# Output projection with the token blocks standing and the weight columns moving

## The chip, the cores and the metric

The kernel runs on one core of one Trainium2 chip. The metric is the device time of one execution in microseconds (us). Three runs of the kernel before took 1353.34, 1355.34 and 1359.38 us; the median is 1355.34. Each number of the trace below comes from one further execution, which was profiled and took 1355.63 us.

The engines are named as in the profile: PE is the matrix engine (PEld its weight loads), DVE the vector engine, ACT the scalar engine, POOL the general one, SP the one that issues most transfers. A matmul has a *standing* operand, which PEld loads into the array, and a *moving* operand, which is streamed through it column by column. A sum of matmuls grows in a PSUM bank (512 fp32 values in each of 128 partitions) and has to be copied out by DVE or ACT.

## What is computed

One decoder layer for a prompt of 512 tokens and a sample group of 32 tokens (8 sequences of 4) with the same weights. An input projection feeds two groups of 8 attention heads each; the heads' outputs, each times a SiLU gate, are joined and go through one output projection, are added to the residual, and are normalised. The part that the change touches:

```python
def merge(x, o_n, z_n, o_f, z_f, w_out):
    mix = jnp.concatenate([o_n * jax.nn.silu(z_n), o_f * jax.nn.silu(z_f)], axis=-1)
    return x + jnp.einsum('btc,cd->btd', mix, w_out)
...
def rmsnorm(x, g):
    xf = x.astype(jnp.float32)
    y = xf * lax.rsqrt(jnp.mean(xf * xf, axis=-1, keepdims=True) + RMS_EPS)
    return (y * g.astype(jnp.float32)).astype(x.dtype)
...
    y_prompt = rmsnorm(hp, norm_final)
    y_sample = rmsnorm(hs, norm_final)
```

`mix` has 2048 columns (16 heads of 128), `w_out` is 2048 by 2048, all in fp32.

## The kernel before

**Precision.** A product of two fp32 matrices is made of three matmuls in the faster type fp32r. Each operand is split into a high part, rounded by a copy on ACT, and a low part, the difference, made by DVE. `mm3` (line 366) issues high x high, high x low and low x high. For the activations the parts are `h_hi` and `h_lo`, [128, 16, 544]: features over the partitions, 16 blocks k of 128 features, and 544 = 512 + 32 tokens. For the weights they are `whi` and `wlo`.

**Projections.** `run_tiles` (452) handles a list of tiles. A tile is 128 columns of a weight matrix, loaded in four pieces of 512 rows (`w_dma`, 417, a ring of five `raw` buffers, 256 KB each) and split two pieces ahead (`w_split`, 437). The weights stand and the tokens move: 544 tokens are cut into two halves of 272 (`cuts`), each half with a PSUM bank of its own (`pz`), and each piece brings 4 k x 3 matmuls to each half. So a tile is 96 matmuls of 272 moving columns, and its result has output features over the partitions and tokens along the row. The evicted result is `zt`, and a generator per tile (`post`) carries on with it.

**Order.** The program is written out by one loop over the tiles, which calls `S.pump()` after every few matmuls. The pump lets the other pieces of work (attention, mixing, eviction) issue their instructions as soon as a model of the engines' clocks, `Clock` (40), thinks that they would not have to wait. Each engine executes its own instructions in that written order. The `Streams` items wait on flags such as `in_done`.

**From the heads to the output.** `post_z` (1605) applies SiLU to a gate tile and leaves it in `mx[:, hd]`. `mix` (1618) multiplies it by the head's output, the prompt part read from `oz`, the sample part from `o_s` [128, 16, 32]. `turn_in` (1634) splits a finished head into `h_hi[:, hd]` and `h_lo[:, hd]`, in place of the input activations, and so waits for `in_done`, the end of all input tiles. The last 16 of the input tiles are the gates z0 to z15.

**Output projection.** Ten tiles of the usual form, then the last six tile columns twice: once for token rows 256 to 543 (288 columns) and once for rows 0 to 255 (`N_TWO = 6`, lines 1742 to 1748), so that half of the tokens can be finished and stored while the other half is still computed. `post_y` (1643) turns each result on PE (five transposes, or three, or two, into `tr` banks), so that tokens lie over the partitions, adds the residual `xr` into `res` [128, 5, 2048] on DVE, sums the squares on ACT, and multiplies by the norm's weight `nfb`. `finish` (1685) forms the root (`rstd_of`, 1712: two operations and four steps of three) for all of a half's token blocks and scales their rows, on DVE and ACT. `store_one` (1708) stores 512 columns of 128 tokens (256 KB) on SP: one store at each weight load for the first half, and the eight of the second half at the end.

Of the kernel before, what the change touches and what calls it, by code (L numbers as in the profile page):

```python
# [1 line left out]

# [5 lines left out]
F32 = mybir.dt.float32  # L8
F32R = mybir.dt.float32r
# [5 lines left out]
P = 128  # L15
# [3 lines left out]
KT = 16  # L19
# [5 lines left out]
N_TWO = 6  # L25
# [248 lines left out]
def trunk_step(ctx, tc, x_prompt, x_sample, cache_nsa_kv, cache_fox_kv, cache_fox_logf, state_nsa_win,  # L274
# [139 lines left out]
    raws, wsp, later = {}, {}, []  # L414
    W_RAW, W_AHEAD = 5, 2

    def w_dma(m):
        t, c = divmod(m, 4)
        if t >= len(tiles):
            return  # L420
        spec = tiles[t]
        raws[m] = raw = wts.tile([P, 4, P], F32, name="raw", bufs=W_RAW)
        src = spec["w"]
        ld = src.shape[-1]
        c = spec.get("rows", (0, 1, 2, 3))[c]
        for (col, n, at) in spec["cols"]:
            nc.sync.dma_start(raw[:, :, at:at + n], dram(src, c * 4 * P * ld + col, [[ld, P], [P * ld, 4], [1, n]]))
        if later:
            store_one()

        b, part = divmod(m - 4 * T_WIN, 4)
        if 0 <= b < 8:
            at = (b * 512 + part * 127) * 512
            nc.sync.dma_start(dram(nsa_win_sample, at, [[512, 127], [1, 512]]),
                              dram(state_nsa_win, at + 4 * 512, [[512, 127], [1, 512]]))

    def w_split(m, part):
        t, c = divmod(m, 4)
        if t == 0 or t >= len(tiles):
            return  # L440
        n = tiles[t]["m"]
        raw = raws[m][:, :, :n]
        if part == 0:
            wsp[m] = [wts.tile([P, 4, P], F32R, name=w, bufs=W_AHEAD + 1) for w in ("whi", "wlo")]
            cp(wsp[m][0][:, :, :n], raw)
        else:
            low(*(x[:, :, :n] for x in wsp[m]), raw)
            del raws[m]
            if m > 4:
                w_dma(m - 1 + W_RAW)  # L450

    def run_tiles(t0, t1):
        for t in range(t0, t1):
# [8 lines left out]
            cuts = spec.get("cuts", ((0, HALF), (HALF, TOK)))  # L462
            ps = [psum.tile([P, b - a], F32, name="pz", tag="pz", bufs=2) for a, b in cuts]
            raw_part = []
            if t >= n_in:
                spec["post"].ahead()
            for c in range(4):
# [19 lines left out]
                if "rows" in spec:  # L487
                    S.need(*[f"h{spec['rows'][c] * 4 + kk}" for kk in range(4)])
                for hf, cut in enumerate(cuts):
                    sl = slice(*cut)  # L490
                    for kk in range(4):
                        k = spec.get("rows", (0, 1, 2, 3))[c] * 4 + kk
                        mm3(ps[hf][:n], (hi[:, kk, :n], lo[:, kk, :n]), (h_hi[:, k, sl], h_lo[:, k, sl]),
                            c == 0 and kk == 0, c == 3 and kk == 3)
                        if kk == 3 and c == 3:

                            if 1 < t < n_in:
                                S.need("rsb")
                            elif t == 1:
                                raw_part.append(sl)  # L500
                            late = max(clock.t["dve"], clock.t["pe"]) > max(clock.t["act"], clock.t["pe"]) + 0.2
                            if not 1 < t < n_in:
                                (cp if late else nc.vector.tensor_copy)(zt[:n, sl], ps[hf][:n])
                            elif late:
                                cp(zt[:n, sl], ps[hf][:n])
                                raw_part.append(sl)
                            else:
                                nc.vector.tensor_tensor(zt[:n, sl], ps[hf][:n], rsb[:n, sl], op=OP.mult)
                        if hf == len(cuts) - 1 and kk % 2 == 0:
                            w_split(m + W_AHEAD, kk // 2)  # L510
                        S.pump()
# [13 lines left out]


# [1091 lines left out]
    def mix(hd):  # L1618
# [12 lines left out]
        nc.vector.tensor_tensor(m[:, SEQ:], m[:, SEQ:], o_s[:, hd, :], op=OP.mult)  # L1631
        flags.add(f"mix{hd}")

    def turn_in(hd):
        yield (f"mix{hd}", "in_done")
        m = MX["mx"][:, hd, :]
        cp(h_hi[:, hd, :], m)
        yield
        low(h_hi[:, hd, :], h_lo[:, hd, :], m)
        flags.add(f"h{hd}")  # L1640


    def post_y(n, r0=0, r1=4, smp=True):

        nr = r1 - r0

        got = []

        def ahead():
            if fin and not got:  # L1650
                got.append(load(fin.tile([P, 4, P], F32, name="xr", bufs=2)[:, :nr],
                                dram(x_prompt, r0 * P * D + n * P, [[D, P], [D * P, nr], [1, P]])))
                if smp:
                    got.append(load(fin.tile([32, P], F32, name="xs", bufs=2), dram(x_sample, n * P, [[D, 32], [1, P]])))

        def f(zt):
            yield "fin"
            ahead()
            xr, xs = got[0], got[-1]
            sl = slice(n * P, (n + 1) * P)  # L1660
            yield from S.take(2)
            psn = tr_tile([P, 4, P])[:, :nr]
            for i in range(nr):
                nc.tensor.transpose(psn[:, i, :], zt[:, (r0 + i) * P:(r0 + i + 1) * P], ident)
            if smp:
                pss = tr_tile([32, P])
                nc.tensor.transpose(pss, zt[:, SEQ:TOK], ident)
            yield
            nc.vector.tensor_tensor(res[:, r0:r1, sl], psn, xr, op=OP.add)
            if smp:  # L1670
                nc.vector.tensor_tensor(res[:32, 4, sl], pss, xs, op=OP.add)
            S.put(2)
            yield
            for i in [*range(r0, r1)] + [4] * smp:
                m = P if i < 4 else 32
                jk = fin.tile([P, P], F32, name="fjk", bufs=2)
                nc.scalar.activation(jk[:m], res[:m, i, sl], AF.Square, accum_out=ssq[:m, i, n:n + 1])
            yield
            nc.vector.tensor_tensor(res[:, r0:r1, sl], res[:, r0:r1, sl], nfb[:, None, sl].to_broadcast([P, nr, P]), op=OP.mult)
            if smp:  # L1680
                nc.vector.tensor_tensor(res[:32, 4, sl], res[:32, 4, sl], nfb[:32, sl], op=OP.mult)
        f.ahead = ahead
        return f

    def finish(r0, r1, smp, last):
        yield tuple(f"post{t}" for t in range(n_in, last + 1))
        a, b = r0, r1 + smp
        n = b - a
        sst, rso, tmo = (fin.tile([P, k * n], F32, name=f"{x}{r0}") for x, k in (("sst", 1), ("rso", 1), ("tmo", 3)))
        nc.vector.tensor_reduce(sst, ssq[:, a:b], axis=AX.X, op=OP.add)  # L1690
        rstd_of(sst, n, rso, tmo)
        yield
        for i in range(a, b):
            m = P if i < 4 else 32
            for q in range(2):
                sl = slice(q * 1024, (q + 1) * 1024)
                if q == 0:
                    nc.vector.tensor_scalar(res[:m, i, sl], res[:m, i, sl], rso[:m, i - a:i - a + 1], None, op0=OP.mult)
                else:
                    nc.scalar.activation(res[:m, i, sl], res[:m, i, sl], AF.Copy, scale=rso[:m, i - a:i - a + 1])  # L1700
                for x in range(2 * q, 2 * q + 2):
                    later.append((y_prompt if i < 4 else y_sample, (i * P * D if i < 4 else 0) + x * 512, m, i, x))
            yield
        if not smp:
            while later:
                store_one()

    def store_one():
        dst, at, m, i, x = later.pop(0)
        nc.sync.dma_start(dram(dst, at, [[D, m], [1, 512]]), res[:m, i, x * 512:(x + 1) * 512])  # L1710

    def rstd_of(ss, n, out, tmp):
        v, y, a = (tmp[:, i * n:(i + 1) * n] for i in range(3))
        nc.vector.tensor_scalar(v, ss, 1.0 / D, 1e-6, op0=OP.mult, op1=OP.add)

        nc.vector.tensor_scalar(y.bitcast(I32), v.bitcast(I32), -0.5, 1597463007.0, op0=OP.mult, op1=OP.add)
        for it in range(4):
            nc.vector.scalar_tensor_tensor(a, y, -0.5, y, op0=OP.mult, op1=OP.mult)
            nc.vector.tensor_tensor(a, a, v, op=OP.mult)
            nc.vector.scalar_tensor_tensor(y if it < 3 else out, a, 1.5, y, op0=OP.add, op1=OP.mult)  # L1720
# [20 lines left out]

    for n in range(KT - N_TWO):
        add_tile(w_out2, [(n * P, P, 0)], post_y(n))
    for rows, cut in (((2, 4, True), (256, TOK)), ((0, 2, False), (0, 256))):
        for n in range(KT - N_TWO, KT):
            add_tile(w_out2, [(n * P, P, 0)], post_y(n, *rows))
            tiles[-1]["cuts"] = (cut,)
        S.add(finish(*rows, len(tiles) - 1))
    for t in range(n_in, len(tiles)):
        tiles[t]["rows"] = (0, 1, 2, 3)  # L1750
# [138 lines left out]
    def last_stage():  # L1889
# [4 lines left out]
        clock.parts[res.tensor.name] = (5 * D, D // 2)  # L1894
        ssq = fin.tile([P, 5, KT], F32, name="ssq")
# [55 lines left out]
    run_tiles(n_in, len(tiles))  # L1951
# [27 lines left out]
```

## Time and profile before

| | us |
|---|---|
| median of three runs | 1355.34 |
| the profiled run | 1355.63 |
| its span, from first to last instruction | 1354.0 |
| first matmul of the output projection, after the span's start | 1132.43 |
| start of its last matmul | 1338.99 |
| issue of the first of the last eight stores | 1345.60 |

A page of the profile gives, in this order, each engine's busy time, 40 slices of the span, the transfers, the chain of work that ended last, and the costliest groups of instructions. Nearly all instructions go through one helper (line 146), so groups are told apart by the names of their tiles: `pz<-h_hi,whi` is a matmul into the bank `pz`, and `128*128 128x272` says that 128 x 128 stand and 128 x 272 move. A row of the timeline has the start, the duration, the engine and the operation; in brackets stand the idle time before it and what ended it. Matmuls overlap one another, so their spacing, not their duration, says what one costs. In the table by windows PEclk is the clock that was granted to PE, 1.00 being full speed.

### The profile page before, as it was taken

To read this page: it belongs to the slowest core of one execution; us is meant where nothing else is said; L and a number is where in the kernel's file an instruction comes from. 1 tells how busy PE (TensorE), PEld (TensorE's weight loads), DVE (VectorE), ACT (ScalarE), POOL (GpSimd) and SP (SyncE) were. 2 spreads that over 40 slices of the span, in tenths; PEclk is the share of its full clock that TensorE was granted. 3 is DMA by queue.
4 is the path that set the end of the run, shared out by engine and by line. 5 is a ranking of instruction groups with operands and counts; after the bars stand their busy time and mean duration, and the time that the engine had idled before them with its cause. 6 is when DMAs were issued, how large, how long until landed. Compare 5 with 4: busy or idle time off the path is not lost.

```text
span 1354.0 us, 28683 instructions
## 1 busy us (share of the span) xinstructions
PE 1291.8 (95%) x10597; PEld 1181.3 (87%) x10597; DVE 799.4 (59%) x1988; ACT 578.9 (43%) x1319; POOL 281.0 (21%) x357
## 2 busy tenths in 40 slices
PE   6989999999998999999999998989999999999995
PEld 4889988889998879999988896756887998999995
DVE  5735778876644446666877854442675646343564
ACT  4313333244432345766543441322466634332563
POOL 3311367733200110000455301212112000000000
PEclk8999999999998999999999998989999999999998
DMA  7576699987646988457688748999897943333565
GB/s 194 148 193 175 187 265 297 270 242 214 172 105 157 307 276 249 139 153 229 202 239 252 217 105 197 285 275 322 224 228 231 298 147 110 109 99 109 148 197 189
DMA packets 383930, 276.02 MB, mean 204 GB/s; under 512 B 119667, under 2 KB 338659, under 8 KB 383117
## 3 DMA queue, kind: packets, MB, share of 16 engines
q1 hardware_dynamic: 359772, 198.09, 53.6%
q0 software_dynamic: 24016, 76.10, 18.1%
q8 instruction: 83, 1.36, 0.4%
q14 instruction: 59, 0.48, 0.1%
HBM read 241.82 MB, written 40.61 MB: 209 GB/s over the span
## 4 chain that ended last, share of the span: by engine, by line
PE 78%; DMA 10%; DVE 4%; SPq 3%; issue 2%; POOL 1%; ACT 1%; ACTq 0%; DVEq 0%; POOLq 0%
PE pz L146 57%; PE tr L146 5%; PE s L146 5%; PE accv L146 5%; PE acc L146 3%; DMA fpg<-in_cache_fox_kv,fi 3%; SPq L146 3%; DMA fpg<-in_cache_fox_kv 2%; PE psb L146 1%; PE accf L146 1%; DMA raw<-in_w_in 1%; DMA xt<-in_x_prompt 1%; POOL fpg L146 1%; DMA spg<-in_cache_nsa_kv 1%; PE pre L146 1%
## 5 line engine op out<-in xcount | busy, mean ns | idle before, releaser
L146 PE MATMUL pz<-h_hi,whi 128*128 128x272 f32 (+2 forms) x2432 | 720.3, 296 | 3.2 <-ACT whi L146 2.3
L146 PE MATMUL pz<-h_hi,wlo 128*128 128x272 f32 (+2 forms) x2432 | 704.8, 290 | 9.5 <-DVE wlo L146 9.5
L146 PE MATMUL pz<-h_lo,whi 128*128 128x272 f32 (+2 forms) x2432 | 702.4, 289 | 1.4 <-DVE h_lo L146 1.4
L146 PEld LDWEIGHTS pz<-h_hi,whi 128*128 128x128 f32 x2432 | 460.5, 189 | 38.5 <-issue 31.8
L146 PEld LDWEIGHTS pz<-h_hi,wlo 128*128 128x128 f32 x2432 | 459.2, 189 | 11.3 <-DVE wlo L146 11.2
L146 PEld LDWEIGHTS pz<-h_lo,whi 128*128 128x128 f32 x2432 | 461.1, 190 | 3.1 <-DVE h_lo L146 2.5
L146 ACT ACTIVATE whi<-raw 128x512 fp32r<-128x512 f32 x328 | 204.4, 625 | 264.5 <-PE pz L146 203.8
L146 DVE TENSOR_TENSOR wlo<-raw,whi 128x512 fp32r<-128x512 f32 x328 | 222.4, 679 | 137.4 <-ACT whi L146 127.9
L146 POOL DMA_INDIRECT fpg<-in_cache_fox_kv,fi x128 | 130.1, 1016 | 222.7 <-ACT nptch L146 144.8
L146 POOL DMA_INDIRECT crow<-in_cache_nsa_kv,ci x64 | 66.5, 1040 | 154.3 <-DVE ct L146 123.5
L146 DVE TENSOR_TENSOR zt<-pz,rsb 128x272 f32<-128x272 f32 x67 | 29.6, 441 | 107.1 <-PE pz L146 107.0
L146 DVE STREAM_TRANSPOSE ft<-fpg 128x1024 f32<-128x1024 f32 x64 | 78.5, 1231 | 22.5 <-DMA fpg<-in_cache_fox_kv,fi 22.4
L146 ACT ACTIVATE cxh<-ct 128x580 fp32r<-128x580 f32 (+1 forms) x64 | 42.3, 660 | 100.3 <-DVE ct L146 96.0
L146 POOL DMA_DIRECT2D fpg<-in_cache_fox_kv x64 | 35.3, 553 | 227.2 <-PE accv L146 166.0
L146 ACT ACTIVATE zt<-pz 128x272 f32<-128x272 f32 (+2 forms) x65 | 25.9, 398 | 113.3 <-PE pz L146 113.1
L146 POOL DMA_DIRECT2D spg<-in_cache_nsa_kv x64 | 35.0, 547 | 132.0 <-DVE skt L146 51.3
L146 DVE TENSOR_TENSOR cxl<-ct,cxh 128x580 fp32r<-128x580 f32 (+1 forms) x64 | 45.9, 717 | 10.1 <-ACT cxh L146 9.6
L146 PE MATMUL accv<-fpg,fpt 128*32 128x512 f32 x256 | 38.8, 631 | 10.5 <-DMA fpg<-in_cache_fox_kv 10.4
L146 ACT ACTIVATE npth<-tr 128x512 fp32r<-128x512 f32 x40 | 23.9, 596 | 49.6 <-PE tr L146 48.1
L146 DVE STREAM_TRANSPOSE ct<-crow 128x512 f32<-128x512 f32 x64 | 44.8, 700 | 0.0
L146 PE MATMUL accv<-ft,fqb 128*32 128x256 f32 x512 | 34.3, 385 | 4.6 <-DVE ft L146 4.6
L146 DVE CUSTOM_DVE_ANT_0 np<-s,nbias 128x128 f32<-128x128 f32 (+1 forms) x64 | 20.2, 352 | 30.7 <-PE s L146 30.7
(384 smaller groups left out, 1622.7 us busy)
## 6 DMA issues: line engine op xcount, KB each, us to landing
raw<-in_w_in SPq DMA_DIRECT2D x240, 256.0 KB
raw<-in_w_out SPq DMA_DIRECT2D x88, 256.0 KB
fpg<-in_cache_fox_kv SPq DMA_DIRECT2D x64, 256.0 KB
fpg<-in_cache_fox_kv POOLq DMA_DIRECT2D x64, 256.0 KB, 6.7
spg<-in_cache_nsa_kv POOLq DMA_DIRECT2D x64, 128.0 KB, 6.8
spg<-in_cache_nsa_kv SPq DMA_DIRECT2D x64, 128.0 KB
spg<-in_state_nsa_win SPq DMA_DIRECT2D x64, 128.0 KB
out<-in_state_nsa_win SPq DMA_DIRECT2D x32, 254.0 KB
```

Of the source, the lines that this page charges most:

```text
L146: return fn(*a, **k)
```

## The change

The output projection leaves `run_tiles` and becomes a loop of its own, `run_outputs`.

- **Operands.** 128 tokens stand (a block i of `h_hi` or `h_lo`), 512 weight columns move. The result has tokens over the partitions at once: `post_y`'s transposes, `finish` and `store_one` are gone.
- **Chunks.** The columns are worked in chunks of 512, 512, 512, 256 and 256. In the first four chunks, the loop goes over the 16 k, and for each k over the four token blocks, each block with its own bank (`bank` goes round all eight banks). The last 256 columns are done block by block (0, sample, 1, 2, 3), each over all 16 k.
- **Sample.** The 32 sample tokens no longer pass through `h_hi` and `h_lo`. They stay in `o_s` in fp32, stand as 32 columns, and the unsplit `raw` weights move in plain fp32; four k go to the four 32-partition groups of one bank, and DVE adds the groups up (`sums`, `i == 4`). In the last 256 columns the high and low weights take the place of the raw ones.
- **Weights.** 64 loads of 256 KB in place of 88. Each load of the first three chunks is one k by 512 columns; the last 512 columns are loaded as pairs of k by 256 columns. A raw tile is kept until the sample has used it, so three more buffers (`rawx`) join the ring. The split weights of the last 256 columns (`wl`) are made during chunks 1 and 2, and lie where `mx` was.
- **Activations.** `turn_in` works on 512 tokens, and may begin with head hd when the last input tile has finished with k blocks 4 (hd // 4) to 4 (hd // 4) + 3 (flags `in0` to `in3`), but at most four heads ahead of chunk 0.
- **End.** Squares of the first 1792 columns are summed as chunks end (`pre`); for the last 256 columns DVE sums them in one operation. The root takes three steps, one block at a time. ACT scales the first 1024 columns, DVE the rest; two stores of 512 KB for each block, both on SP, but for block 3, whose second is issued by ACT.

```diff
     def w_dma(m):
         t, c = divmod(m, 4)
-        if t >= len(tiles):
+        if t >= n_in:
+            j = m - 4 * n_in
+            loaded[0] = m + 1
+            if j % 8 < 5:
+                raws[m] = raw = wts.tile([P, 4, P], F32, name="raw", bufs=W_RAW)
+            else:
+                raws[m] = raw = fin.tile([P, 4, P], F32, name="rawx", bufs=3)
+            flat = raw.rearrange("p a b -> p (a b)")
+            nc.sync.dma_start(flat if out_steps[j][0] < 3 else flat.rearrange("p (a b) -> p a b", a=2), out_src(j))
             return
...
+    def run_outputs():
+        order = cycle((("pz", 2), ("pz", 2), ("s", 2), ("s", 2), ("acc", 1), ("accv", 1), ("tr", 2), ("tr", 2)))
...
+        def sums(ch, i, ps, xr, xs):
+            c0, w = ((0, 512), (512, 512), (1024, 512), (1536, 256), (1792, 256))[ch]
...
+            nc.vector.tensor_tensor(r, ps[:m], xr[i][:, x0:x0 + w] if i < 4 else xs[:, x0:x0 + w], op=OP.add)
+            for q in range(1, 4 if i == 4 else 1):
+                if ch < 4:
+                    yield free("dve")
+                nc.vector.tensor_tensor(r, ps[q * 32:q * 32 + 32], r, op=OP.add)
+            if ch < 4:
+                yield free("act")
+                jk = stg.tile([P, TOK], F32, name="zt", bufs=2)
+                nc.scalar.activation(jk[:m, :w], r, AF.Square, accum_out=ssq[:m, i, ch:ch + 1])
+                yield free("dve")
+                nc.vector.tensor_tensor(r, r, nfb[:m, sl], op=OP.mult)
...
+                return
+            yield lambda: i in pre
...
+            nc.vector.tensor_tensor_reduce(jk[:m, :w], r, r, 1.0, 0.0, OP.mult, OP.add, accum_out=ss)
...
+            rstd_of(ss, 1, rso[:m], tmo[:m], 3, pre[i][:m, 1:])
+            yield [rso]
...
+            nc.scalar.activation(a, a, AF.Copy, scale=rso[:m])
+            nc.vector.tensor_scalar(res[:m, i, HALF_D:c0], res[:m, i, HALF_D:c0], rso[:m], None, op0=OP.mult)
+            nc.vector.scalar_tensor_tensor(r, r, rso[:m], nfb[:m, sl], op0=OP.mult, op1=OP.mult)
+            yield [b]
+            nc.sync.dma_start(dram(dst, at + HALF_D, [[D, m], [1, D - HALF_D]]), b)
+            yield [a]
+            (nc.scalar if i == 3 else nc.sync).dma_start(dram(dst, at, [[D, m], [1, HALF_D]]), a)
...
+        def residual(c):
+            xr = [load(MX["pl"].tile([P, SEQ], F32, name="oz", bufs=4), dram(x_prompt, i * P * D + c * 512, [[D, P], [1, 512]])) for i in range(4)]
+            cols[c] = xr, load(fin.tile([32, 512], F32, name="xs", bufs=2), dram(x_sample, c * 512, [[D, 32], [1, 512]]))
+
+        def loads():
+            while state["load"] - m0 < len(out_steps) and state["load"] - 8 not in raws:
+                w_dma(state["load"])
+                state["load"] += 1
...
+        def smp(ps, parts, first, last):
+            for q, (k, w) in enumerate(parts):
+                mm(ps[q * 32:q * 32 + 32], o_s[:, k], w, first, last)
...
+        for ch in range(4):
+            w = 512 if ch < 3 else 256
+            n = 512 // w
+            ps = [bank(w) for _ in range(5)]
+            ms = []
+            for step in range(16 // n):
...
+                hi, lo = (x.rearrange("p a b -> p (a b)") for x in wsp.pop(m))
+                todo = ahead(m)
+                loads()
+                for kk in range(n):
+                    k = step * n + kk
+                    if ch == 0:
+                        S.need(f"h{k}")
...
+                    if k == 12:
+                        residual(ch)
...
+                    for i in range(4):
+                        sl = slice(i * P, (i + 1) * P)
+                        mm3(ps[i], (h_hi[:, k, sl], h_lo[:, k, sl]), (hi[:, wsl], lo[:, wsl]), k == 0, k == 15)
+                        if k == 15:
+                            S.add(sums(ch, i, ps[i], *cols[ch]), front=True)
...
+                g, at = divmod(step, 4 // n)
+                if at == 4 // n - 2:
...
+                    smp(ps[4], parts, g == 0, g == 3)
...
+        for i in (0, 4, 1, 2, 3):
+            ps = bank(256)
+            if i == 4:
+                for k in range(0, KT, 2):
+                    smp(ps, [(k + y, wl[:, x, k + y].bitcast(F32)) for y in range(2) for x in range(2)], k == 0, k == KT - 2)
+            else:
+                sl = slice(i * P, (i + 1) * P)
+                for k in range(KT):
+                    mm3(ps, (h_hi[:, k, sl], h_lo[:, k, sl]), (wl[:, 0, k], wl[:, 1, k]), k == 0, k == KT - 1)
...
     def turn_in(hd):
-        yield (f"mix{hd}", "in_done")
-        m = MX["mx"][:, hd, :]
-        cp(h_hi[:, hd, :], m)
+        yield (f"mix{hd}", f"in{hd // 4}")
+        yield lambda: hd < last_w.get("k", 0) + 5
+        m = MX["mx"][:, hd, :SEQ]
+        cp(h_hi[:, hd, :SEQ], m)
         yield
-        low(h_hi[:, hd, :], h_lo[:, hd, :], m)
+        low(h_hi[:, hd, :SEQ], h_lo[:, hd, :SEQ], m)
         flags.add(f"h{hd}")
```

More of the change, by code (lines that the diff above doesn't have):

```diff
@@ L1 @@
 from contextlib import ExitStack, contextmanager
+from itertools import cycle
 import concourse.bass as bass
@@ L24 @@
 FPG = 2
-N_TWO = 6
+HALF_D = 1024
 T_WIN = 28
@@ L413, in trunk_step, with out_steps_kind, out_src @@
     tiles = []
-    raws, wsp, later = {}, {}, []
-    W_RAW, W_AHEAD = 5, 2
+    raws, wsp, last_w, loaded = {}, {}, {}, [0]
+    out_steps = []
+    for ch in range(3):
+        for k in range(KT):
+            out_steps.append((ch, k))
+            if ch and k % 4 == 3:
+                out_steps.append((4, 4 * (ch - 1) + k // 4))
+    out_steps += [(3, i) for i in range(8)]
+    W_RAW, W_AHEAD = 5, 2
+    def out_steps_kind(m):
+        j = m - 4 * n_in
+        return out_steps[j][0] if j < len(out_steps) else -1
+    def out_src(j):
+        kind, i = out_steps[j]
+        if kind < 3:
+            return dram(w_out2, i * P * D + kind * 512, [[D, P], [1, 512]])
+        return dram(w_out2, 2 * i * P * D + 1536 + (kind - 3) * 256, [[D, P], [P * D, 2], [1, 256]])
     def w_dma(m):
         t, c = divmod(m, 4)
-        if t >= len(tiles):
+        if t >= n_in:
+            j = m - 4 * n_in
+            loaded[0] = m + 1
[5 more added lines that the diff above has]
+            nc.sync.dma_start(flat if out_steps[j][0] < 3 else flat.rearrange("p (a b) -> p a b", a=2), out_src(j))
             return
@@ L424, in w_dma @@
         ld = src.shape[-1]
-        c = spec.get("rows", (0, 1, 2, 3))[c]
         for (col, n, at) in spec["cols"]:
             nc.sync.dma_start(raw[:, :, at:at + n], dram(src, c * 4 * P * ld + col, [[ld, P], [P * ld, 4], [1, n]]))
-        if later:
-            store_one()
         b, part = divmod(m - 4 * T_WIN, 4)
@@ L438, in w_split @@
         t, c = divmod(m, 4)
-        if t == 0 or t >= len(tiles):
+        if t == 0 or m >= 4 * n_in + len(out_steps):
             return
-        n = tiles[t]["m"]
+        n = tiles[t]["m"] if t < n_in else P
         raw = raws[m][:, :, :n]
         if part == 0:
-            wsp[m] = [wts.tile([P, 4, P], F32R, name=w, bufs=W_AHEAD + 1) for w in ("whi", "wlo")]
+            if t >= n_in and out_steps[m - 4 * n_in][0] == 4:
+                i = out_steps[m - 4 * n_in][1]
+                if "w" not in last_w:
+                    wl = MX["pl"].tile([P, 2, 16, 256], F32R, name="wl", tag="mx")
+                    clock.parts[wl.tensor.name] = (2 * 16 * 256, 512)
+                    last_w["w"] = wl
+                wsp[m] = [last_w["w"][:, x, 2 * i:2 * i + 2, :].rearrange("p a b -> p (a b)").rearrange("p (a b) -> p a b", b=P)
+                          for x in range(2)]
+            else:
+                wsp[m] = [wts.tile([P, 4, P], F32R, name=w, bufs=W_AHEAD + 1) for w in ("whi", "wlo")]
             cp(wsp[m][0][:, :, :n], raw)
@@ L447, in w_split @@
             low(*(x[:, :, :n] for x in wsp[m]), raw)
-            del raws[m]
-            if m > 4:
-                w_dma(m - 1 + W_RAW)
+            if t < n_in:
+                del raws[m]
+                if m > 4:
+                    w_dma(m - 1 + W_RAW)
     def run_tiles(t0, t1):
@@ L461, in run_tiles @@
             clock.parts[zt.tensor.name] = (TOK, HALF)
-            cuts = spec.get("cuts", ((0, HALF), (HALF, TOK)))
+            cuts = ((0, HALF), (HALF, TOK))
             ps = [psum.tile([P, b - a], F32, name="pz", tag="pz", bufs=2) for a, b in cuts]
             raw_part = []
-            if t >= n_in:
-                spec["post"].ahead()
             for c in range(4):
@@ L486, in run_tiles @@
                 hi, lo = wsp.pop(m)
-                if "rows" in spec:
-                    S.need(*[f"h{spec['rows'][c] * 4 + kk}" for kk in range(4)])
                 for hf, cut in enumerate(cuts):
@@ L491, in run_tiles @@
                     for kk in range(4):
-                        k = spec.get("rows", (0, 1, 2, 3))[c] * 4 + kk
+                        k = c * 4 + kk
                         mm3(ps[hf][:n], (hi[:, kk, :n], lo[:, kk, :n]), (h_hi[:, k, sl], h_lo[:, k, sl]),
@@ L495, in run_tiles @@
                         if kk == 3 and c == 3:
-                            if 1 < t < n_in:
+                            if t > 1:
                                 S.need("rsb")
@@ L501, in run_tiles @@
                             late = max(clock.t["dve"], clock.t["pe"]) > max(clock.t["act"], clock.t["pe"]) + 0.2
-                            if not 1 < t < n_in:
+                            if t == 1:
                                 (cp if late else nc.vector.tensor_copy)(zt[:n, sl], ps[hf][:n])
@@ L510, in run_tiles @@
                             w_split(m + W_AHEAD, kk // 2)
+                        if hf == len(cuts) - 1 and kk == 3 and t == n_in - 1:
+                            flags.add(f"in{c}")
                         S.pump()
@@ L1630, in mix @@
         yield "nsas" if hd < 8 else f"foxs{(hd - 8) // 4}"
-        nc.vector.tensor_tensor(m[:, SEQ:], m[:, SEQ:], o_s[:, hd, :], op=OP.mult)
+        nc.vector.tensor_tensor(o_s[:, hd, :], m[:, SEQ:], o_s[:, hd, :], op=OP.mult)
         flags.add(f"mix{hd}")
     def turn_in(hd):
-        yield (f"mix{hd}", "in_done")
-        m = MX["mx"][:, hd, :]
-        cp(h_hi[:, hd, :], m)
+        yield (f"mix{hd}", f"in{hd // 4}")
+        yield lambda: hd < last_w.get("k", 0) + 5
+        m = MX["mx"][:, hd, :SEQ]
@@ L1638, in turn_in @@
+        cp(h_hi[:, hd, :SEQ], m)
         yield
-        low(h_hi[:, hd, :], h_lo[:, hd, :], m)
+        low(h_hi[:, hd, :SEQ], h_lo[:, hd, :SEQ], m)
         flags.add(f"h{hd}")
[L1643 to L1712, printed above, removed]
+    def rstd_of(ss, n, out, tmp, steps=4, more=None):
         v, y, a = (tmp[:, i * n:(i + 1) * n] for i in range(3))
-        nc.vector.tensor_scalar(v, ss, 1.0 / D, 1e-6, op0=OP.mult, op1=OP.add)
+        if more is None:
+            nc.vector.tensor_scalar(v, ss, 1.0 / D, 1e-6, op0=OP.mult, op1=OP.add)
+        else:
+            nc.vector.scalar_tensor_tensor(v, ss, 1.0 / D, more, op0=OP.mult, op1=OP.add)
@@ L1716, in rstd_of @@
         nc.vector.tensor_scalar(y.bitcast(I32), v.bitcast(I32), -0.5, 1597463007.0, op0=OP.mult, op1=OP.add)
-        for it in range(4):
+        for it in range(steps):
             nc.vector.scalar_tensor_tensor(a, y, -0.5, y, op0=OP.mult, op1=OP.mult)
             nc.vector.tensor_tensor(a, a, v, op=OP.mult)
-            nc.vector.scalar_tensor_tensor(y if it < 3 else out, a, 1.5, y, op0=OP.add, op1=OP.mult)
+            nc.vector.scalar_tensor_tensor(y if it < steps - 1 else out, a, 1.5, y, op0=OP.add, op1=OP.mult)
@@ L1740, in trunk_step @@
     n_in = len(tiles)
[L1742 to L1750, printed above, removed]
     def start():
@@ L1893, in last_stage @@
         res = fin.tile([P, 5, D], F32, name="res")
-        clock.parts[res.tensor.name] = (5 * D, D // 2)
-        ssq = fin.tile([P, 5, KT], F32, name="ssq")
+        clock.parts[res.tensor.name] = (5 * D, 256)
+        ssq = fin.tile([P, 5, 5], F32, name="ssq")
+        clock.parts[ssq.tensor.name] = (25, 5)
         nfb = load(fin.tile([P, D], F32, name="nfb"), dram(norm_final, 0, [[0, P], [1, D]]))
@@ L1950, in trunk_step @@
         S.need("mx")
-    run_tiles(n_in, len(tiles))
+    run_outputs()
     S.drain()
```

62 lines of the change are left out of this document (added).

## The prediction

> **What bounds the kernel now.** I read the page first, then the output stage in the table by windows, then its start and end in the timeline.
>
> ```profile
> span 1354.0 us, 28683 instructions
> PE 1291.8 (95%) x10597; PEld 1181.3 (87%) x10597; DVE 799.4 (59%) x1988; ACT 578.9 (43%) x1319; POOL 281.0 (21%) x357
> PE 78%; DMA 10%; DVE 4%; SPq 3%; issue 2%; POOL 1%; ACT 1%; ACTq 0%; DVEq 0%; POOLq 0%
> ```
> ```profile
> core 0: us, PE busy (x) PEld busy (x) DVE busy (x) ACT busy (x) POOL busy (x), PEclk, DMA share, GB/s
> 1132.43:1150.00 17.57, 15.25 (x110) 13.76 (x109) 14.78 (x25) 9.94 (x18) 0.00 (x0) 1.00 0.28 83
> 1150.00:1264.00 114.00, 114.00 (x915) 113.88 (x913) 47.09 (x91) 35.91 (x126) 0.00 (x0) 1.00 0.37 106
> 1264.00:1302.00 38.00, 38.00 (x292) 37.94 (x291) 22.34 (x47) 21.77 (x68) 0.00 (x0) 1.00 0.60 174
> 1302.00:1339.10 37.10, 36.45 (x307) 36.19 (x305) 23.99 (x55) 22.28 (x57) 0.00 (x0) 1.00 0.72 221
> 1339.10:1354.00 14.90, 0.61 (x4) 0.20 (x2) 5.05 (x20) 2.88 (x6) 0.00 (x0) 0.63 0.38 141
> ```
>
> PE owns 78% of the chain. From 1150 to 1302 it never rests, while DVE and ACT are busy under two thirds of each window. So the stage costs what its matmuls cost; only its first 18 us and the last 14.9 us, where the final norm and the stores run alone, hold waits. The change touches this stage alone (1132.43 to 1354.0, 221.6 us); what runs before it is issued as before.
>
> **The price of a column.** Matmuls overlap, so I count start to start, not durations.
>
> ```profile
> 1126.78 0.28 PE L146 MATMUL pz<-h_hi,whi 128*128 128x272 f32 x1
> ...
> 1132.31 0.29 PE L146 MATMUL pz<-h_hi,wlo 128*128 128x272 f32 x1
> 1132.43 0.28 PE L146 MATMUL pz<-h_hi,whi 128*128 128x272 f32 x1
> 1133.76 0.39 PE L146 MATMUL pz<-h_lo,whi 128*128 128x272 f32 x1 [1.04 <-DVE h_lo L146]
> ...
> 1146.02 0.39 PE L146 MATMUL pz<-h_hi,whi 128*128 128x272 f32 x1 [0.91 <-ACT h_hi L146]
> ...
> 1149.78 0.71 PE L146 MATMUL tr<-ident,zt 128*128 128x128 f32 x5
> 1150.24 0.37 PE L146 MATMUL pz<-h_hi,whi 128*128 128x272 f32 x1
> ```
> ```profile
> 1311.31 0.38 PE L146 MATMUL pz<-h_hi,wlo 128*128 128x256 f32 x1 [0.65 <-DVE wlo L146]
> ...
> 1311.64 0.28 PE L146 MATMUL pz<-h_lo,whi 128*128 128x256 f32 x1
> ...
> 1315.91 0.29 PE L146 MATMUL pz<-h_lo,whi 128*128 128x256 f32 x1
> ```
> ```profile
> 1068.82 0.39 PE L146 MATMUL tr<-fkh,fqh 128*128 128x512 f32 x1
> ...
> 1069.52 0.28 PE L146 MATMUL accf<-fpth,fvh 128*128 128x256 f32 x1
> ```
>
> 44 steps of 272 columns take 5.53 us: 0.1257 each. 36 of 256 take 4.27: 0.1186. Three of 512 take 0.70: 0.233, of which I take 0.232. That is 0.46 ns a column at 256 and 272, and 0.453 at 512: width alone saves 2%. At 0.46 ns, 288 columns cost 0.132.
>
> **What goes.** Ten tiles of 96 matmuls (120.7 us), six of 48 at 288 (38.0), six of 48 at 256 (34.2): 192.9 us. Then the turning of the result on TensorE: five transposes hold 0.46 us, with the slow restart behind them 0.55, for each of ten tiles, and some 0.3 for each of the twelve narrow ones: 9.1 us. Sum 202. The stage ran from 1132.43 to 1339.11, the end of its last 256-column matmul: 206.7 us. The other 4.7 are waits, such as the 1.04, 0.91 and 0.65 above.
>
> **What comes for the prompt.** Tokens stand, weight columns move: 3 chunks x 16 k x 4 token blocks x 3 = 576 matmuls of 512, and two times 192 of 256. 576 x 0.232 = 133.6; 384 x 0.1186 = 45.5; together 179.1. It is 13.8 us less, mostly because the 32 sample tokens (6% of the columns) no longer pass three times.
>
> **What comes for the sample.** Plain fp32 matmuls, 32 tokens standing, four k in four column groups. The form is in the trace:
>
> ```profile
> 929.80 0.61 PE L146 MATMUL acc<-spg,PT 128*32 128x256 f32 x8
> 930.34 0.39 PE L146 MATMUL pz<-h_hi,whi 128*128 128x272 f32 x1
> ...
> 930.70 0.29 PE L146 MATMUL pz<-h_hi,wlo 128*128 128x272 f32 x1
> 930.91 1.06 PE L146 MATMUL accv<-fpg,fpt 128*32 128x512 f32 x8
> 931.91 0.40 PE L146 MATMUL pz<-h_hi,whi 128*128 128x272 f32 x1
> 932.14 0.29 PE L146 MATMUL pz<-h_lo,whi 128*128 128x272 f32 x1
> ```
>
> Eight of 512 hold PE 1.00 us, eight of 256 0.54: 0.08 fixed and 0.46 for 2048 columns. Going in costs 0.21 in place of 0.126, coming out 0.23: 0.19 a visit. Four of 512 are then 0.73, twelve times: 8.8. Four of 256: 0.50, four times: 2.0. The last visit, 32 of 256 (high and low weights apart): 2.1. Together 12.9 us, 8 if the visits themselves cost nothing.
>
> **Waits.** A k of chunk 0 lasts 12 x 0.232 = 2.8 us.
>
> ```profile
> L146 ACT ACTIVATE h_hi<-mx x16: 640/642/656, 1130.0 to 1145.3; 128x544 fp32r<-128x544 f32 x16
> L146 DVE TENSOR_TENSOR h_lo<-mx,h_hi x16: 715/717/726, 1133.0 to 1146.0; 128x544 fp32r<-128x544 f32 x16
> ```
>
> A head's copy and difference (0.64 and 0.72 us) now have 2.8, and those of heads 0 to 3 are issued one quarter into the last input tile, 72 matmuls or 9 us earlier, on engines with time to spare (43% and 59% busy over the span). The 16th, ready at 1146, is wanted at about 1174. So the start's waits go. What is late next is the bank: block 1 of chunk 0 takes the bank that DVE empties after the last input matmul, a few tenths. I leave 1.0 us for all waits; the bounds are 0 and the 4.7 of today. DVE, busy 113 of the 221 us by the windows above, loses 24 of 88 weight splits and gains the sums over the sample's four groups: beside PE, at no cost. The five residual loads of a chunk pass through SP at k = 12, some 11 us before the first sum wants them; should they be late, only DVE waits, since the next chunk has its own banks.
>
> 192.0 + 1.0 us from 1132.43: the last matmul starts at 1325.3, not 1338.99.
>
> **The end.**
>
> ```profile
> 1338.99 0.28 PE L146 MATMUL pz<-h_hi,wlo 128*128 128x256 f32 x1
> 1339.31 0.42 DVE L146 COPY zt<-pz 128x256 f32<-128x256 f32 x1 [2.70 <-PE pz L146]
> ...
> 1342.06 0.17 DVE L146 TENSOR_SCALAR tmo<-sst 128x2 f32<-128x2 f32 x1
> ...
> 1344.82 1.42 DVE L146 TENSOR_SCALAR res<-res,rso 128x1024 f32<-128x1024 f32 x2
> 1344.88 2.19 ACT L146 ACTIVATE res<-res,rso 128x1024 f32<-128x1024 f32 x2 [3.40 <-DVE rso L146]
> 1345.60 4.47 SPq L146 DMA_DIRECT2D out<-res  x8
> ```
> ```profile
> L146 DVE CUSTOM_DVE_ANT_1 jkd<-xt 128x2048 f32<-128x2048 f32 x1 | 2.3, 2286 | 0.0
> ```
>
> Today the end is 15.0 us: eviction, transposes, sum, squares, 14 small operations at 0.197 (1342.06 to 1344.82), scaling, and eight stores of 256 KB that end 8.4 us after the first is issued. The new end has one block of 128 tokens: 0.32 to DVE, the sum 0.35, the square of 256 columns 0.45 (an estimate: an eighth of 2.29 and a fixed part), 11 small operations 2.17, half a row scaled on ACT 1.14 with DVE's 1.0 beside it, hops 0.1: 4.5 us. Then two stores of 512 KB, on SP and ACT, with nothing queued behind them. The last of today's eight is issued at 1349.5 (eight in 4.47) and lands 4.5 us later; 4.5 and 8.4 bound it, and half the bytes on two queues is near the first: 5.2. The new end is 9.7 us, 5.3 less.
>
> **Sum.** 1325.3 + 9.7 = 1335.0 against 1354.0: 19.0 us less. The profiled run took 1355.63, that is 1.6 beside its span and 0.3 over the median of 1355.34. Predicted: 1355.3 - 19.0 = **1336**.
>
> **Rivals.**
>
> ```profile
> 420.00:424.00 4.00, 3.88 (x17) 3.88 (x18) 2.47 (x6) 1.51 (x3) 0.00 (x0) 0.50 0.47 131
> ```
> ```profile
> fpg<-in_cache_fox_kv POOLq DMA_DIRECT2D x64, 256.0 KB, 6.7
> ```
>
> *Weights come late (10%).* A raw tile now stays until the sample has used it, and SP stands in order behind that. A reload is issued one step after its group's visit, wanted by ACT about 7 us and by PE about 11 us later; the nearest landing time is 6.7 us. If each of 16 groups cost PE the 0.65 to 1 us that it waited for wlo at 1311, 10 to 16 us go back: 1346 to 1352. Against it: the stage moves little more than the 106 GB/s above.
>
> *Column groups run one after another (5%).* A block of four would take four times its 0.46: 72 matmuls' worth of 512 columns x 0.345 = 24.8 us more: 1361, no change that can be told. The rows at 930.91 speak against it.
>
> *The clock falls (4%, slower).* From 420 to 424, after PE had waited 4 us, the granted clock was 0.50: 2 us lost each time. Each of the 17 visits changes mode and bank; if each set this off, 34 us are lost: 1370. It decides from about ten such falls, a mean clock of 0.91. Against it: from 1132 to 1150, with waits of 1 us, the clock stayed 1.00. The Trainium skill, TensorE: Matmul & The Clock Gate, under "A second HAM failure mode: psum-queue depth-cycling", says that cycling through banks can make the clock swing; by it this rival would be likely, and the rows at 930, which change bank and mode without a fall, do not bear it out.
>
> *Wide streams cost less (6%).* If in long runs the 2% at 512 grew to 5%, 0.224 each, 5 us more are won: 1331. The same page, under "Back-to-back issue gap", gives N/2.4 + 2.5 ns, 216 ns for 512; the sum would be 1324. The trace disagrees already at 256, with 118.6 where that gives 109.
>
> **How the numbers follow.** Forecast 72%, its own range 1330 to 1344: waits +3.7 or -1, end -1 to +3 (DVE has about 4 us of work a block and 5.7 us for it, so a block may be late), visits -5. The rivals hold 25%; 3% stay for some other loss. The range reaches into the late weights: 1329 to 1347. A measurement can tell about 0.5%, 6.8 us. Faster by more (below 1348.6): forecast, wide streams and a part of late weights, 0.81; same 0.13; slower 0.06.
>
> **What would show it.** Right: 512-column matmuls 0.23 apart; visits of about 0.7 us, 16 small and one long; no wait for h_lo after the input tiles; 9 to 11 us behind the last matmul. Wrong: gaps before matmuls put down to wlo or a weight load, a granted clock under 0.95 between 1132 and 1325, visits of 2 us, or DVE still at block 2 when block 3 ends.

## The result, and the profile after

The changed kernel took 1345.65 us (median of five runs, 1343.14 to 1346.19) beside 1359.38 for the kernel before in five runs of the same session (1355.34 in the three that were known ahead). The ratio is 0.9909, with a 95% interval of 0.9885 to 0.9933: faster by 0.9%, some 12 us, where 19 were forecast. The profiled run took 1346.01 us, 9.6 less than the profiled run of before. Run again on another chip, where both kernels take some 5% longer, the ratio was 0.9867 (0.9809 to 0.9924).

The page after, its first lines and the chain by engine:

```profile
span 1344.2 us, 27395 instructions
PE 1289.9 (96%) x10133; PEld 1138.4 (85%) x10133; DVE 787.6 (59%) x1977; ACT 548.2 (41%) x1164; POOL 278.5 (21%) x357
PE 74%; DMA 11%; SPq 4%; issue 3%; DVE 3%; POOL 3%; ACT 1%; POOLq 0%; DVEq 0%; ACTq 0%
```

The output stage after, by windows (length, busy time of each engine with its instructions, granted clock of PE, share of the DMA engines, GB/s):

```profile
1134.45:1200.00 65.55, 65.55 (x297) 48.24 (x296) 30.68 (x49) 23.72 (x45) 0.00 (x0) 1.00 0.31 102
1200.00:1309.00 109.00, 109.00 (x602) 84.35 (x601) 44.62 (x72) 30.43 (x62) 0.00 (x0) 1.00 0.36 116
1309.00:1334.70 25.70, 25.70 (x258) 23.90 (x257) 19.25 (x85) 6.47 (x14) 0.00 (x0) 1.00 0.27 99
1334.70:1344.20 9.50, 0.14 (x2) 0.00 (x0) 3.62 (x16) 1.15 (x1) 0.00 (x0) 0.70 0.52 206
```

PE does not rest between the first and the last matmul, and its clock stays at 1.00. Outside the visits to the sample, each matmul starts within 0.25 us of the one before it, but for one that starts 0.33 us after it at the second block of chunk 0. So, but for that 0.1 us, nothing waits for weights, banks or heads; whatever the stage takes too long is in the matmuls themselves. Three marks divide the span (us; the stage runs from the start of its first matmul to the end of its last, what lies behind from the start of the last to the end of the span):

| | before | forecast | after |
|---|---|---|---|
| first matmul of the output stage | 1132.43 | 1132.4 | 1134.45 |
| stage | 206.7 | 193.0 | 200.2 |
| behind the last matmul | 15.0 | 9.7 | 9.6 |
| span | 1354.0 | 1335.0 | 1344.2 |

The end came out as worked out. The stage is 7.2 us longer than forecast. The start is 2.0 us later, with the same PE instructions in the same order ahead of it. Here is a visit to the sample in chunk 0, and the long one in the last 256 columns:

```profile
1142.72 0.40 PE L147 MATMUL po<-whi,h_lo 128*128 128x512 f32 x1
1143.04 1.06 PE L147 MATMUL po<-raw,o_s 128*32 128x512 f32 x8
1144.04 0.50 PE L147 MATMUL po<-whi,h_hi 128*128 128x512 f32 x1
1144.38 0.40 PE L147 MATMUL po<-wlo,h_hi 128*128 128x512 f32 x1
...
1149.98 0.39 PE L147 MATMUL po<-wlo,h_hi 128*128 128x512 f32 x1
```
```profile
1314.43 0.28 PE L147 MATMUL po<-wl,h_lo 128*128 128x256 f32 x1
1314.64 3.66 PE L147 MATMUL po<-wl,o_s 128*32 128x256 f32 x64
1318.23 0.39 PE L147 MATMUL po<-wl,h_hi 128*128 128x256 f32 x1
```

The program issues four fp32 matmuls in the first of these visits, and the trace has eight rows; it issues 32 in the second, and the trace has 64. The visit takes as long as eight rows did before, 1.00 us, for half the work that I had counted.

From 1144.38 to 1149.98 lie 24 steps: 0.2333 for 512 columns.

### The profile page after: what moved, and what is told of

Read it like the earlier page. It is cut to its first block, busy times and chain, and to the rows that moved or that the text cites. A ratio compares the mean times of both kernels' runs of the same rounds, so it can differ in the third digit from the quotient of the medians.

```text
span 1344.2 us, 27395 instructions
## 1 busy us (share of the span) xinstructions
PE 1289.9 (96%) x10133; PEld 1138.4 (85%) x10133; DVE 787.6 (59%) x1977; ACT 548.2 (41%) x1164; POOL 278.5 (21%) x357
## 4 chain that ended last, share of the span: by engine, by line
PE 74%; DMA 11%; SPq 4%; issue 3%; DVE 3%; POOL 3%; ACT 1%; POOLq 0%; DVEq 0%; ACTq 0%
PE pz L147 40%; PE po L147 15%; PE s L147 5%; PE accv L147 4%; PE tr L147 4%; SPq L147 4%; PE acc L147 3%; DMA spg<-in_cache_nsa_kv 2%; DMA fpg<-in_cache_fox_kv,fi 2%; POOL fpg L147 2%; DMA fpg<-in_cache_fox_kv 1%; PE psb L147 1%; PE accf L147 1%; DMA xt<-in_x_prompt 1%; DMA raw<-in_w_in 1%
## 5 line engine op out<-in xcount | busy, mean ns | idle before, releaser
L147 PE MATMUL pz<-h_hi,whi 128*128 128x272 f32 x1920 | 572.2, 298 | 2.3 <-ACT whi L147 2.3
L147 PE MATMUL pz<-h_hi,wlo 128*128 128x272 f32 x1920 | 557.9, 291 | 10.0 <-DVE wlo L147 9.9
L147 PE MATMUL pz<-h_lo,whi 128*128 128x272 f32 x1920 | 556.1, 290 | 0.0
L147 PEld LDWEIGHTS pz<-h_hi,whi 128*128 128x128 f32 x1920 | 365.4, 190 | 37.3 <-issue 31.9
L147 PEld LDWEIGHTS pz<-h_hi,wlo 128*128 128x128 f32 x1920 | 364.5, 190 | 11.1 <-DVE wlo L147 11.1
L147 PEld LDWEIGHTS pz<-h_lo,whi 128*128 128x128 f32 x1920 | 365.9, 191 | 0.6
L147 PE MATMUL po<-whi,h_hi 128*128 128x512 f32 (+1 forms) x256 | 95.6, 373 | 0.0
L147 PE MATMUL po<-wlo,h_hi 128*128 128x512 f32 (+1 forms) x256 | 93.9, 367 | 0.0
L147 PE MATMUL po<-whi,h_lo 128*128 128x512 f32 (+1 forms) x256 | 93.8, 367 | 0.0
L147 PEld LDWEIGHTS po<-wlo,h_hi 128*128 128x128 f32 x256 | 48.2, 188 | 8.1
```

The source lines that it names most:

```text
L147: return fn(*a, **k)
```

## The experiments

**Theory A**: an fp32 matmul is two rows of the trace, so the sample costs 21.0 us where 12.9 were priced. For a visit of four at 512 columns that is 1.00, and 0.09 + 0.10 for going in (0.32 to 0.33 in place of 0.233) and out (0.34 in place of 0.233): 1.19, twelve times 14.3; four of 0.72 at 256 columns, 2.9; the long one 3.8. (The four at 256 columns take 0.76 each in the trace, 0.57 and 0.19 around it. That is 0.2 us more in all; the 21.0 is kept, as the expectations below use it.) **Rivals**: the missing time is in the prompt's own matmuls, or the 17 changes between the two forms cost more than priced.

The runs of the first four experiments come from one chip and those of the repetition from another, and on both everything before the output stage takes longer (1431 us for the kernel before). Each experiment is one run. So I compare the stage, between its own marks, and not the spans.

**Three quarters of the sample's matmuls left out.** The sample's output is then not complete; only the time is read.

```diff
-                    smp(ps[4], parts, g == 0, g == 3)
+                    if g == 0:
+                        smp(ps[4], parts, True, True)
...
-                for k in range(0, KT, 2):
+                for k in range(0, 4, 2):
-                    smp(ps, [(k + y, wl[:, x, k + y].bitcast(F32)) for y in range(2) for x in range(2)], k == 0, k == KT - 2)
+                    smp(ps, [(k + y, wl[:, x, k + y].bitcast(F32)) for y in range(2) for x in range(2)], k == 0, k == 2)
```

> Leaves out three quarters of the sample's output projection: one visit of four k in each of the first four chunks instead of four, and 4 instead of 16 k in the last 256 columns. Theory A (an fp32 matmul of the sample is two rows of the trace, so a visit of four costs 1.19 us, not 0.73, and the sample 21.0 us in all): the time from the first to the last matmul of the output stage falls by 9 x 1.19 + 3 x 0.72 + 2.7 = 15.6 us, from 200.2 to about 184.6. Prices of the prediction (12.9 us for the sample, the other 8 us lost by the prompt's own matmuls): by 9.7 us, to about 190.5.

First and last matmul of its stage, from the timeline:

```profile
1194.70 0.40 PE L147 MATMUL po<-whi,h_hi 128*128 128x512 f32 x1
...
1379.08 0.28 PE L147 MATMUL po<-wl,h_lo 128*128 128x256 f32 x1
```

184.4 us between the two starts, 184.5 to the end: 15.7 less than after the change, where A gave 15.6 and the prediction's prices 9.7. The sample's matmuls and the changes of form around them do cost what A says. The prompt's matmuls are not where the time went.

**Each of the sample's matmuls issued twice in its visit.**

```diff
-                    smp(ps[4], parts, g == 0, g == 3)
+                    for again in (False, True):
+                        smp(ps[4], parts, g == 0 and not again, g == 3 and again)
```

and the same in the last 256 columns.

> Issues each of the sample's fp32 matmuls a second time inside the same visit, so that the sample's sums are wrong by the repeated products. The number of visits stays. Theory A (two rows per matmul, the matmuls themselves are dear): 12 x 0.92 + 4 x 0.46 + 3.6 = 16.5 us more, the stage at about 216.7. Rival B (the matmuls cost what the prediction said and the missing 8 us are the 17 changes of mode): 8.3 us more, about 208.5.

```profile
1204.06 0.40 PE L147 MATMUL po<-whi,h_hi 128*128 128x512 f32 x1
...
1212.64 1.92 PE L147 MATMUL po<-raw,o_s 128*32 128x512 f32 x16
...
1419.60 0.28 PE L147 MATMUL po<-wl,h_lo 128*128 128x256 f32 x1
```

The stage takes 215.7 us, 15.4 more (A: 16.5; B: 8.3). Eight matmuls, 16 rows, last 1.92 us where four last 1.06: 0.86 for four of 512 columns, where A had 0.92, and 0.14 of the visit's 1.00 that does not grow with the matmuls. So of the 21.0 us the matmuls themselves are 15.4 and the 17 visits as such 5.6, 0.33 each. B falls: the changes of form cost little more than the 0.27 (0.19 and 0.08) of the prediction. Of the 8.1 us that the prediction lacked, 7.1 are the matmuls (15.4 in place of 8.3) and 1.0 the visits (5.6 in place of 4.6).

**The sample as a fifth block of standing tokens.** Its 32 tokens are split into high and low parts again and go through `mm3` with the weights that move for the prompt, in the last 256 columns too; the sums over four groups fall away.

```diff
-                    for i in range(4):
-                        sl = slice(i * P, (i + 1) * P)
-                        mm3(ps[i], (h_hi[:, k, sl], h_lo[:, k, sl]), (hi[:, wsl], lo[:, wsl]), k == 0, k == 15)
+                    for i in range(5):
+                        sl = slice(i * P, min(TOK, (i + 1) * P))
+                        mm3(ps[i][:P if i < 4 else 32], (h_hi[:, k, sl], h_lo[:, k, sl]), (hi[:, wsl], lo[:, wsl]), k == 0, k == 15)
```

> Undoes the sample's part of the change alone: the sample's 32 tokens are split into high and low and stand as a fifth block of 32 columns in the same three fp32r matmuls with the same moving weights. If a matmul costs by its moving columns whatever stands, the sample costs 48 x (3 x 0.234 + 0.118 + 0.114) = 44.8 us instead of 21.0: the stage at about 224, the span some 24 us longer than after the change. If 32 standing columns cost a quarter, 11.2 us, and the stage is at about 190.

```profile
1214.91 0.40 PE L147 MATMUL po<-whi,h_hi 128*128 128x512 f32 x1
...
1217.81 0.40 PE L147 MATMUL po<-whi,h_hi 128*32 128x512 f32 x1
1218.04 0.39 PE L147 MATMUL po<-wlo,h_hi 128*32 128x512 f32 x1
1218.27 0.39 PE L147 MATMUL po<-whi,h_lo 128*32 128x512 f32 x1
1218.50 0.39 PE L147 MATMUL po<-whi,h_hi 128*128 128x512 f32 x1
...
1438.02 0.28 PE L147 MATMUL po<-wl,h_lo 128*128 128x256 f32 x1
```

The stage takes 223.2 us, 23.0 more; a matmul with 32 standing columns takes 0.23 us like one with 128. Once the tokens stand, plain fp32 in four column groups is the better of the two ways for the sample that were run, by 23 us. It is only dearer than I had priced it.

**The kernel before without the sample's columns.**

```diff
             cuts = spec.get("cuts", ((0, HALF), (HALF, TOK)))
+            if t >= n_in:
+                cuts = tuple((a, min(b, SEQ)) for a, b in spec.get("cuts", ((0, 256), (256, SEQ))))
```

> The kernel before, with the 32 sample columns left out of the matmuls of the output tiles (halves of 256 in place of 272, and 256 in place of 288); the sample's output is not computed. It gives the price of the sample in the old form: 32 columns x 48 x 16 x 0.457 ns = 11.2 us less, the stage at 195.5 instead of 206.7. If so, the sample alone is 10 us dearer in the new form, and the prompt alone falls from 195.5 to 179. Rival: the prompt's matmuls do not get cheaper by the turning of the operands, and the stage falls by far more than 11 us. It also shows how far the start of the output stage wanders between two executions of the same input part (1132.4 in the profile of before): by theory about 2 us either way.

```profile
1202.30 0.27 PE L146 MATMUL pz<-h_hi,whi 128*128 128x256 f32 x1
...
1203.63 0.39 PE L146 MATMUL pz<-h_lo,whi 128*128 128x256 f32 x1 [1.05 <-DVE h_lo L146]
...
1399.64 0.28 PE L146 MATMUL pz<-h_hi,wlo 128*128 128x256 f32 x1
```

The stage takes 197.5 us, 9.2 less than with the sample; 11.2 were expected. By their spacing in the traces (0.1258 for 272 columns, 0.1321 for 288, 0.1188 for 256) the matmuls alone fall by some 10.5, and the waits and turns between them take some 1 us more. This divides the change in two: with the sample's columns left out the stage fell from 197.5 to 200.2 - 21.0 = 179.2, by 18.3 us; what these columns add to it rose from 9.2 to 21.0, by 11.8. The net is the 6.5 that the two traces show (206.7 to 200.2). But the sample's transposes, 16 of the 80, are still issued in this experiment. At the 0.46 us for five of the prediction they are some 1.5 us (an estimate), which belong to the sample in the old form: so some 17 us were won for the prompt, and some 10 lost for the sample.

**The last 256 columns by k, all four blocks together,** the sample first.

```diff
-        for i in (0, 4, 1, 2, 3):
+        for i in (4, 0):
...
-                sl = slice(i * P, (i + 1) * P)
+                pk = [ps] + [bank(256) for _ in range(3)]
                 for k in range(KT):
-                    mm3(ps, (h_hi[:, k, sl], h_lo[:, k, sl]), (wl[:, 0, k], wl[:, 1, k]), k == 0, k == KT - 1)
-                    if k % 4 == 3:
+                    for x in range(4):
+                        sl = slice(x * P, (x + 1) * P)
+                        mm3(pk[x], (h_hi[:, k, sl], h_lo[:, k, sl]), (wl[:, 0, k], wl[:, 1, k]), k == 0, k == KT - 1)
...
```

> Undoes one part: the last 256 columns go over k with the four token blocks inside, as in the chunks before, instead of block by block; the sample goes first. All four blocks then end within 1.1 us. By the prediction's price (some 4 us of DVE for each block's end) the root and scaling of four blocks queue on DVE, 16 us, and the time behind the last matmul grows from 9.6 to about 21 us; the matmuls cost the same. If the stores or ACT set the end instead, four blocks of 1 MB at some 300 GB/s end about 14 to 15 us behind the last matmul. If nothing queues: 11.

Its timeline around the last matmul and at the end:

```profile
1334.26 0.28 PE L147 MATMUL po<-wl,h_lo 128*128 128x256 f32 x1
...
1334.94 0.28 PE L147 MATMUL po<-wl,h_lo 128*128 128x256 f32 x1
...
1337.28 1.15 ACT L147 ACTIVATE res<-res,rso 128x1024 f32<-128x1024 f32 x1 [14.79 <-DVE rso L147]
...
1345.88 0.16 DVE L147 SCALAR_TENSOR_TENSOR rso<-tmo 128x1 f32<-128x1 f32 x1
1345.95 0.61 DVE L147 TENSOR_SCALAR res<-res,rso 128x768 f32<-128x768 f32 x1
...
1346.99 7.13 SPq L147 DMA_DIRECT2D out<-res  x7
```

The matmuls take the same 200.2 us. The end takes 25.1 us in place of 9.6: the four roots queue on DVE until 1346.0, no row is scaled by DVE before that, and 4 MB of stores start at 1347.0 and need until 1360.0. The queue on DVE was expected; that the stores then have to go all at once behind it, 13 us, was not in the 21. Part of that is the order in which the program is written: ACT has scaled the first half of one block's rows at 1338.4, but SP stores the half that DVE scales first, and DVE scales only behind all four roots. Another order was not run. Against this one, going block by block is worth 15.5 us; with the end of this experiment, and the same stage, the kernel would be slower than before. It took 1361.80 us beside 1354.72 for the kernel before, one run each.

**The heads' split waits for the end of all input tiles again.**

```diff
-        yield (f"mix{hd}", f"in{hd // 4}")
+        yield (f"mix{hd}", "in_done")
```

> Undoes one part: the split of the mixed heads into the activations' high and low parts waits for the end of all input tiles again. The first matmul of the output stage then waits for one copy and one difference, 0.64 + 0.72 us and hops; after that a head has 2.8 us and is ready in 0.7. Expected 1.3 to 1.7 us between the last input matmul and the third of the output stage, and no further wait: the early start is worth about 1.5 us of the 4.7 that the stage of before waited, the slower pace the rest. Rival: the early start holds up nothing and is worth nothing, or the whole 4.7 us come back.

```profile
1135.84 0.40 PE L147 MATMUL po<-whi,h_hi 128*128 128x512 f32 x1
...
1137.14 0.50 PE L147 MATMUL po<-whi,h_lo 128*128 128x512 f32 x1 [0.66 <-DVE h_lo L147]
```

One wait, and the stage is 0.8 us longer (201.1). The third matmul, which is the first to want the low part, starts 1.30 us after the first in place of 0.47. The early start is worth 0.8, not the 1.5 expected: the third matmul would start 0.47 us behind the first in any case. Of the 4.7 us that the sum put down to waits before, the profile gives 2.3 to waits for the heads' parts, 0.7 to a weight and 0.5 to a transpose. That the rest of the 2.3 went with the slower pace at which heads are asked for is likely, since nothing else waits here, but no run changes the pace alone.

**Both kernels once more, on one chip.**

> The kernel before once more, on the same chip as the next run. The input part of both kernels has the same PE instructions in the same order, so theory says: the output stage's first matmul (1132.43 in the profile of before, 1134.45 in that after) wanders by a few us from execution to execution and is not tied to the kernel; the stage itself (206.7 us) and what follows its last matmul (15.0 us) repeat within 0.3 us. Rival: the changed kernel starts its output stage 2 us later because of the change.

> The changed kernel once more on that chip. Stage 200.2 us and end 9.6 us as before within 0.3; its first matmul within 4 us of the run beside it, earlier or later. By stage and end alone (206.7 + 15.0 - 200.2 - 9.6 = 11.9 us) the ratio should be 0.991.

Of before, then of after, the first and the last matmul of the stage:

```profile
1206.72 0.28 PE L146 MATMUL pz<-h_hi,whi 128*128 128x272 f32 x1
...
1413.28 0.28 PE L146 MATMUL pz<-h_hi,wlo 128*128 128x256 f32 x1
```
```profile
1192.36 0.40 PE L147 MATMUL po<-whi,h_hi 128*128 128x512 f32 x1
...
1392.47 0.28 PE L147 MATMUL po<-wl,h_lo 128*128 128x256 f32 x1
```

Stages of 206.7 and 200.2 us and ends of 15.0 (1413.28 to the span's 1428.3) and 9.6 us (1392.47 to 1402.1): both repeat to a tenth, on a chip whose start of the stage is 58 to 74 us later. So stage and end are worth 6.5 + 5.4 = 11.9 us, 0.9%.

The start itself was 14 us *earlier* here with the changed kernel, and 2 us later in the first pair of traces. Both differences arise while the two programs still issue the same: the last 581 matmuls before the stage take 73.10 us in each of the ten traces, and in the first pair the first instruction that differs between the programs (the sample's product, now left in `o_s`) runs at 1071.2 us, 63 us before the stage. Whether the kernel as a whole still moves the start is open. With the lengths of stage and end taken off each run's span, the stage starts at 1130 to 1138 us in five runs of before and at 1131 to 1135 in five of after in the first session, but at 1198 to 1213 in eight of before and at 1192 to 1200 in four of after on this chip. That is why the ratio there is lower than stage and end give; the runs do not show why.

## Why the prediction was right in kind and wrong in size

- **The price of the sample: wrong, and this is the step that failed.** "Eight of 512 hold PE 1.00 us" took eight rows for eight matmuls. They are four matmuls. "Four of 512 are then 0.73, and there are 12 visits" should have been 1.19, and the term 21.0 and not 12.9: 8.1 us too little. The trace of before could have shown it. The first input tile uses the same form: the source issues, for each of four pieces and two halves, four matmuls with `h_hi`, 32 in all, and the view of that tile's name counts 64.

```profile
L146 PE MATMUL pz<-h_hi,ft x64: 389/393/534, 14.1 to 32.0; 128*32 128x272 f32 x64
```

- **The prompt's matmuls: right, the last digit by luck.** 512 columns take 0.2333 to 0.234 us (0.232 taken), 256 in chunk 3 0.118 (0.1186 taken) and 0.113 in the last columns. 576 x 0.234 + 192 x 0.118 + 192 x 0.113 = 179.1; forecast 179.1. The wide ones are 1.1 us dearer and the narrow ones 1.2 cheaper than priced, and the two misses cancel.
- **Waits: right, even better.** 1.0 us was left for them; about 0.1 is seen, at the second block of chunk 0.
- **The end: right.** 9.7 forecast, 9.6 measured. Its parts, after the last matmul's start at 1334.57: the sum begins 0.31 later, the root is ready after 3.3, ACT has scaled at 4.5, the last store is issued at 4.55 and lands 5.1 later. The block-by-block order is what makes it so short, as the experiment by k shows.

```profile
1334.88 0.42 DVE L147 TENSOR_TENSOR res<-po,oz 128x256 f32<-128x256 f32 x1 [1.36 <-PE po L147]
...
1337.74 0.16 DVE L147 SCALAR_TENSOR_TENSOR rso<-tmo 128x1 f32<-128x1 f32 x1
1337.94 1.15 ACT L147 ACTIVATE res<-res,rso 128x1024 f32<-128x1024 f32 x1 [4.28 <-DVE rso L147]
...
1339.12 0.37 ACTq L147 DMA_DIRECT2D out<-res  x1
```

- **The sum.** 1335.0 + 8.1 (sample) - 0.9 (waits) + 2.0 (start of the stage, which wanders) = 1344.2, the span that was measured. The forecast's own range, 1330 to 1344, did not hold the measured 1345.65; the wider one of 1329 to 1347 did, by luck, with room that had been meant for late weights.
- **The rivals.** Late weights: no wait for a weight is left in the stage. Column groups one after another: no; eight rows of 0.6 us each take 1.00 together. A falling clock: no, banks change every three matmuls for 174 us and the granted clock is 1.00 in each window of the stage. The Trainium skill, TensorE: Matmul & The Clock Gate, under "A second HAM failure mode: psum-queue depth-cycling", tells of a kernel in which PE idles often between groups of matmuls while it cycles through banks, and the clock swings; here PE does not idle, so this case doesn't test it. Cheaper wide streams: no, 512 columns take 0.2333 us. The same page, under "Back-to-back issue gap", gives 216 ns for 512 columns; the measured 233 decides here.

## What to carry to other kernels

Before a row of the trace is used as the price of one instruction, count the instructions in the source and the rows in the view of the same tile: a form may be recorded as two rows, and then half the price comes out. Give the parts of a change that are not alike a term and an experiment each; here the turned operands won some 17 us for the prompt and the sample's new form gave some 10 of them back, which no total shows. In a stage bound by one engine, let the last columns end one block after another: the work behind the last matmul is then that of one block.

## What the runs showed of the hardware

- An fp32 matmul with 32 standing and 512 moving columns is two rows of the trace; four of them in four column groups take 0.86 us, and a visit to this form costs 0.33 us beside them (0.09 going in, 0.10 coming out, 0.14 that does not grow with the matmuls).
- An fp32r matmul with 512 moving columns takes 0.23 us, with 32 as with 128 standing columns.
- 256-column matmuls run at 0.113 us in the last columns, and at 0.118 in chunk 3 and 0.1186 before. That a block's matmuls all go to one bank there is not the reason: by k, with the bank changed every three matmuls, the six steps from 1334.26 to 1334.94 take 0.113 each too. The runs do not show what is.
- The output stage's first matmul comes at 1132 to 1136 us in the four traces from the faster chips and at 1192 to 1215 in the six from the two slower ones. It differs by 9 us between two runs on one chip with the same program ahead of it (1194.70 and 1204.06, the first two experiments), while the stage that is bound by PE repeats to 0.1 us.
